# A gated two-branch layer: the output projection by seven products on halves, with the bias added to the input in DRAM

## The chip, the cores and the metric

The kernel runs on one core of a Trainium2 chip. The metric is the device time of one execution in microseconds (us), the median of several runs. The engines of the core are TensorE (PE: matrix products; its weight loads are shown apart as PEld), VectorE (DVE), ScalarE (ACT), GpSimd (POOL) and SyncE (SP). SP and POOL also issue DMA transfers, each through a queue of its own. "L389" stands at nearly every instruction of the profile, because a planner issues all of them from that one line; instructions are told apart by the tiles that they write and read.

## What is computed

The sizes are 1024 time steps (SEQ), 1024 channels (D_MODEL), one layer, float32 throughout. Cut to what matters here:

```python
h = x @ w_in + b_in                                   # 1024 x 6144
xa, za, xb, zb, ga, gb = split(h)                     # 1024 channels each
ya = rg_lru(causal_conv4(xa)) * silu(za)
yb = multiscale_pool(xb) * silu(zb)
merged = sigmoid(ga) * (ya @ w_proj_a) + sigmoid(gb) * (yb @ w_proj_b)
y = merged @ w_out + b_out                            # the output projection
out = layer_norm(alpha * x + y, ln_gain, ln_bias)     # alpha = 2 ** 0.25, mean and variance over the channels
```

## The kernel before

A float32 product is made of three matmuls: each operand is split into a high part in the matmul's own format (a cast on ScalarE) and the rest (a subtraction on VectorE, together `split`), and high x high, high x low and low x high are summed in a PSUM bank. One matmul takes a 128 x 128 block as weights and 512 columns as the moving operand.

Three stages follow one another on TensorE. In the first, the 24 groups of `order` (line 592: kinds A, G and B for the two branches and the gates) form `x @ w_in`, each by seven products on halves of the matrices in place of eight; the gate matmuls and the pooling run between them. `ya` and `yb` go to DRAM. In the second, the merge (from line 1188), the two projections are formed step by step, branch a and then branch b, each again by seven products (`steps`, line 1190: a in the order 1, 2, 6, 5, 3, 7, 4, then b in the order 1, 2, 6, 7, 5, 4, 3). A step is four groups `g` of twelve matmuls; its operands are loaded by `load` two steps ahead and split by `cast` one step ahead. The four quarters of `merged` lie in `sums[d // 2, h]` (d: block of 128 channels, h: half of the time steps); a quarter is complete when branch b's part is added, after b's steps 2, 5, 4 and 3 (`DONE`, line 1218). `split_m` (line 1239) then splits each block of it.

The sums of weights and inputs that the seven products need are made in DRAM by copies and adding DMAs on the POOL queue. They wait in a list (`jobs`, line 649), first in, first out. `run_jobs` (line 654) takes one after an A group and two after a G or B group, and each time POOL first copies one number that ScalarE copies out of the group (`pace`), so that the jobs don't run ahead. The list holds the sums of both projections' weights (`weight_sums`), the first and second part of the sums of ya (`input_sums1`, `input_sums2`, queued when its blocks 3 and 7 are stored) and the same of yb; the second part of yb is taken up in merge step ("a", 3).

The third stage is the output projection with the layer norm (from line 1338). It has no halves: for each block `s` of 128 time steps and each half `e` of the output columns `o_mm` (line 1357) sums over all eight channel blocks, 24 matmuls into one bank. First come eight blocks with e = 0, then eight with e = 1; the last bank is made in two pieces of 256 columns. `z` holds alpha * x + b_out, made by VectorE from a loaded x. `o_evac` (line 1365) adds the bank to z and takes the statistics of the sum (BATCH_NORM_STATS2); `o_norm` (line 1371) aggregates them, ScalarE takes the root, and four multiplies on VectorE (two for mean and gain, two for deviation and bias, 512 columns each) and two stores end a block. The weights of e = 0 are loaded and cast during the merge (`CASTS`, line 1281), those of e = 1 after it.

The order on every engine is set ahead of time by the planner (`Plan`, lines 162 to 397): TensorE and POOL keep the order of the program, and for the others a list schedule with guessed costs takes the task that is due first. A task is due when the first matmul that depends on it is, or, if none does, 40 us after its place in the program (1 us if it reads a PSUM bank or a tile of the small pool `e`). A task that becomes ready up to 3 us later and is due earlier makes a less urgent one wait (`HOLD`, line 361). Tiles come from pools with fixed numbers of buffers: 28 of kind x, 10 of kind w, 4 of kind r, 10 of kind k, 4 of kind e and 8 PSUM banks; a task that writes a new tile waits until one is free.

Of the kernel before, what the change touches and what calls it, by code (L numbers as in the profile page):

```python
# [16 lines left out]
P = 128  # L17
# [144 lines left out]
class Plan:  # L162
# [22 lines left out]
    def add(self, name, eng, op, args, kw):  # L185
# [6 lines left out]
        t.ins = refs[1:] if t.outs else refs  # L192
        t.deps, t.users, t.new = set(), [], []
# [61 lines left out]
    def order(self):  # L255
# [26 lines left out]
        state = {"table": None, "SP": 0.0, "ACT": 0.0, "POOL": 0.0, "pe": 0}  # L282
# [17 lines left out]
        def begin(t, now):  # L300
# [4 lines left out]
            t.start = now  # L305
            free[t.eng] = now + t.time
# [21 lines left out]
        while done < len(T):  # L328
            moved = True
            while moved:  # L330
# [10 lines left out]
                for e in ("ACT", "DVE", "SP", "POOL"):  # L341
# [60 lines left out]
def layer_kernel(ctx: ExitStack, tc: tile.TileContext, xq, x, w_in, par, wg, w_pool, wpa, wpb, w_out, rows, out):  # L402
# [324 lines left out]
    def a_gates(c, xc, xh, xl, sz):  # L727
# [388 lines left out]
    for i in range(1, len(order)):  # L1116
# [51 lines left out]
        if i >= 2:  # L1168
            run_jobs(1 if kind == "A" else 2, i, g.t7)
# [63 lines left out]
    sums, mh, ml = {}, {}, {}  # L1233
    HOMES = {2: (kt, kt), 5: (kt, xt), 4: (xt, rt), 3: (xt, xt)}
# [4 lines left out]
    def split_m(j, d, h):  # L1239
        if d % 2 == 0:  # L1240
            for k, t in enumerate((mh, ml)):
                f = HOMES[j][k]
                t[d // 2, h] = f(f"m{k}{d}{h}", F32R) if f is not kt else f(f"m{k}{d}{h}", F32R).rearrange("p (g s) -> p g s", g=2)
        sign = 1.0 if d < KQ else -1.0
        A.mul(of(mh, d, h), of(sums, d, h), sign)
        V.scalar_tensor_tensor(of(ml, d, h), of(sums, d, h), sign, of(mh, d, h).bitcast(F32), ALU.mult, ALU.subtract)

    wo = {}

    raw_wo = {}  # L1250


    def load_wo(e, p):
        raw_wo[e, p] = kt(f"wor{e}_{p}").rearrange("p (k n) -> p k n", k=2)
        nc.sync.dma_start(raw_wo[e, p], w_out[2 * p * P:2 * (p + 1) * P, e * H:(e + 1) * H].rearrange("(k p) n -> p k n", p=P))

    def cast_wo(e, p):
        h, l = ((wt if e == 0 else xt)(f"wo{t}{e}_{p}") for t in "hl")
        split(raw_wo.pop((e, p)), h, l)
        for k in range(2):  # L1260
            wo[e, 2 * p + k] = (h[:, k, :], l[:, k, :])
# [20 lines left out]
    for i, (n, j) in enumerate(steps):  # L1282
# [10 lines left out]
        for g in range(KQ):  # L1293
# [17 lines left out]
            if (n, j) in DONE:  # L1311
# [26 lines left out]
    for p in range(KQ):  # L1338
        load_wo(1, p)
        cast_wo(1, p)  # L1340
    rb = []
    for i in range(3):
        t = xt(f"row{i}", F32, (P, S))
        nc.sync.dma_start(t, rows[i:i + 1, :].to_broadcast((P, D)))
        rb.append(t)
    b_row, g_row, be_row = rb
    zt, stats = [], []
    for s in range(NK):
        t = xt(f"z{s}", F32, (P, S))
        nc.sync.dma_start(t, x[s * P:(s + 1) * P, :])  # L1350
        V.scalar_tensor_tensor(t, t, ALPHA, b_row, ALU.mult, ALU.add)
        zt.append(t)
        stats.append(const.tile([P, 4 if s == NK - 1 else 2, 6], F32, name=f"stats{s}"))
    eps = const.tile([P, 1], F32, name="eps")
    nc.gpsimd.memset(eps, EPS)

    def o_mm(ps, s, e, ks, sl=slice(0, H)):
        for k in ks:
            wh, wl = (w[:, sl] for w in wo[e, k])
            h, c = divmod(s * P, H)  # L1360
# [93 lines left out]
```

## Time and profile before

| | us |
|---|---|
| median of 3 runs (754.29 to 754.6) | 754.5 |
| the profiled execution, whole | 754.04 |
| its span, first to last instruction | 752.2 |
| TensorE busy | 742.5 (99%) |
| VectorE busy | 598.4 (80%) |
| ScalarE busy | 432.2 (57%) |
| GpSimd busy | 54.5 (7%) |

The profile is of one execution. Matmuls overlap in the pipeline, so one shows 389 ns while one starts about every 227 ns; the number of slots is what fills TensorE's time. The stage of the output projection runs from 656.42 us to the end. "Idle before" is an engine's idle time just ahead of an instruction, with what ended it.

### The profile page before, as it was taken

Reading aid. Unit: us, or ns where it says so; the run is one execution under the profiler, and the core shown is the slowest. Engines: PE = TensorE matmul, PEld = TensorE weight load, DVE = VectorE, ACT = ScalarE, POOL = GpSimd, SP = SyncE. Lnnn points to the kernel's source line nnn. Section 1 sums busy time; section 2 is a strip of 40 time slices with the busy share of each in tenths; the row PEclk is TensorE's granted clock in tenths of the full one; section 3 lists DMA queues with packets and bytes.
Section 4 is the critical chain, followed back from the end, with each engine's and each line's share of the span. In section 5 each row is a group of like instructions: output and inputs, shape, how many; then the busy total and the mean of one; then the engine's idle time right before and its main releaser. Section 6 shows DMA issues by size and latency. Waiting matters only on the chain.

```text
span 752.2 us, 8755 instructions
## 1 busy us (share of the span) xinstructions
PE 742.5 (99%) x3308; PEld 608.6 (81%) x3308; DVE 598.4 (80%) x740; ACT 432.2 (57%) x556; POOL 54.5 (7%) x101
## 2 busy tenths in 40 slices
PE   9999999999999999999999999999999999999996
PEld 6887888888788878878888888888888888888885
DVE  7898695959595969699977768779958896977587
ACT  7676969597787777788665444465543654230000
POOL 0160010101010100010011001000000000000000
PEclk9999999999999999999999999999999999999998
DMA  9146567657566647254278526898599996181022
GB/s 343 64 145 156 179 159 198 166 175 195 147 163 198 166 176 173 85 171 142 80 161 171 112 76 176 309 382 270 197 300 302 330 295 220 57 315 48 29 93 103
DMA packets 54730, 135.90 MB, mean 181 GB/s; under 512 B 3936, under 2 KB 7136, under 8 KB 54624
## 3 DMA queue, kind: packets, MB, share of 16 engines
q1 hardware_dynamic: 41248, 99.43, 37.9%
q0 software_dynamic: 12896, 35.65, 21.4%
q8 instruction: 26, 0.43, 0.2%
q10 hardware_dynamic: 544, 0.26, 0.1%
q14 instruction: 16, 0.13, 0.1%
HBM read 114.36 MB, written 56.62 MB: 227 GB/s over the span
## 4 chain that ended last, share of the span: by engine, by line
PE 95%; ACT 2%; DVE 1%; DMA 1%; issue 0%; DVEq 0%; ACTq 0%
PE ps_o L389 12%; PE a_B L389 11%; PE a_A L389 10%; PE a_G L389 10%; PE pa_a L389 6%; PE pa_b L389 6%; PE c_A L389 6%; PE c_B L389 5%; PE c_G L389 4%; PE ps_pool L389 3%; PE pc_b L389 3%; PE pc_a L389 3%; PE e_A L389 3%; PE ps_s L389 3%; PE e_G L389 3%; PE e_B L389 3%
## 5 line engine op out<-in xcount | busy, mean ns | idle before, releaser
L389 PE MATMUL ps_o<-woh,m 128*128 128x512 f32 (+1 forms) x272 | 80.5, 379 | 0.0
L389 ACT ACT_TABLE_LOAD x39 | 50.0, 1283 | 42.8 <-DVE mv L389 40.1
L389 PEld LDWEIGHTS ps_o<-woh,m 128*128 128x128 f32 x272 | 50.1, 188 | 10.1
L389 PE MATMUL ps_o<-wol,m 128*128 128x512 f32 (+1 forms) x136 | 51.5, 378 | 0.0
L389 DVE TENSOR_TENSOR i<-i,xc 128x1024 f32<-128x1024 f32 x8 | 9.8, 1225 | 38.6 <-ACT i L389 38.6
L389 POOL COPY paced<-pace 128x1 f32<-128x1 f32 x19 | 13.4, 706 | 259.6 <-ACT pace L389 259.6
L389 DVE SCALAR_TENSOR_TENSOR xc<-xp,par_sb,xc 128x1024 f32<-128x1024 f32 x24 | 30.8, 1282 | 0.5
L389 PEld LDWEIGHTS ps_o<-wol,m 128*128 128x128 f32 x136 | 25.6, 188 | 5.0
L389 DVE TENSOR_TENSOR z<-ps_o,z 128x512 f32<-128x512 f32 (+1 forms) x17 | 11.2, 659 | 18.8 <-PE ps_o L389 18.3
L389 PE MATMUL pa_a<-oh,oh 128*128 128x512 f32 x64 | 24.9, 389 | 0.0
L389 PE MATMUL pa_a<-oh,ol 128*128 128x512 f32 x64 | 24.9, 389 | 0.0
L389 PE MATMUL pa_a<-ol,oh 128*128 128x512 f32 x64 | 24.9, 389 | 0.0
L389 PE MATMUL pa_b<-oh,oh 128*128 128x512 f32 x64 | 24.9, 389 | 0.0
L389 PE MATMUL pa_b<-ol,oh 128*128 128x512 f32 x64 | 24.9, 389 | 0.0
L389 PE MATMUL pa_b<-oh,ol 128*128 128x512 f32 x64 | 24.9, 389 | 0.0
L389 ACT ACTIVATE m<-m 128x512 fp32r<-128x512 f32 x16 | 10.1, 632 | 25.3 <-DVE m L389 25.3
L389 ACT ACTIVATE i<-ps_g,par_sb 64x512 f32<-64x512 f32 x32 | 21.9, 685 | 3.3 <-DVE r L389 2.8
L389 ACT ACTIVATE sd<-mv,eps 128x1 f32<-128x1 f32 x8 | 2.4, 295 | 34.9 <-DVE mv L389 34.9
L389 ACT ACTIVATE r<-ps_g,par_sb 64x512 f32<-64x512 f32 x32 | 21.9, 684 | 0.5
L389 ACT ACTIVATE zb<-zb,par_sb 128x1024 f32<-128x1024 f32 (+1 forms) x16 | 14.9, 937 | 10.7 <-DVE zb L389 10.3
L389 PE MATMUL c_B<-x64h,wd_B 128*128 128x512 f32 x64 | 21.0, 389 | 0.0
L389 PE MATMUL c_A<-x64h,wd_A 128*128 128x512 f32 x64 | 21.0, 389 | 0.0
(435 smaller groups left out, 2380.9 us busy)
## 6 DMA issues: line engine op xcount, KB each, us to landing
sg<-sg SPq DMA_DIRECT2D x16, 512.0 KB, 3.6
ra_A<-in_w_in SPq DMA_DIRECT2D x8, 512.0 KB, 4.9
rb_A<-in_w_in SPq DMA_DIRECT2D x8, 512.0 KB, 3.8
ya<-r SPq DMA_DIRECT2D x8, 512.0 KB, 2.9
ra_B<-in_w_in SPq DMA_DIRECT2D x8, 512.0 KB, 3.4
rb_B<-in_w_in SPq DMA_DIRECT2D x8, 512.0 KB, 3.7
yb<-zb SPq DMA_DIRECT2D x8, 512.0 KB, 6.0
sgla<-sg SPq DMA_DIRECT2D x8, 512.0 KB, 6.3
```

The lines of the kernel that those rows point to most:

```text
L389: getattr(getattr(nc, t.op[0]), t.op[1])(*a, **k)
```

## The change

It replaces the third stage and what feeds it.

- The output projection becomes seven products on halves of `merged` and `w_out`, in the order 1, 6, 7, 5, 3, 4, 2 (`O_STEPS`), each four groups of twelve matmuls. Products 1, 6, 5 and 3 share the banks `a`, 7 and 4 the banks `c`; 2 has banks of its own, and its last group is made in two pieces of 256 columns. After products 1, 6, 7 and 5 the partial results are added to z as well, so a half block of z gets one to three adds in place of one.
- The sums of the weights are made in DRAM by eight more jobs (`output_sums`), queued when block 3 of ya is stored. The sums of `merged` are made on VectorE (`o_sums`, `o_sum4`), six operations of 1024 columns and two more. Of the splits of `merged` those of one quarter stay in the merge (`o_first`); the others become twelve splits of 1024 columns (`o_input`).
- b_out / alpha is added to x in DRAM by eight more jobs (`biased_input`, queued when block 7 of ya is stored), and the factor alpha goes into the first add. `run_jobs` takes two jobs after A and G groups and three after B groups.
- Except in the last block, the row sums come out of the adds (`accum_out`), and the sum of squares out of a Square on ScalarE over the whole block; BATCH_NORM_STATS2 goes there. The last block keeps its statistics.
- In the planner, a second output (`accum_out`) is tracked, and the test that makes a less urgent task wait takes account of how late TensorE is (`lag`).

```diff
+        if isinstance(kw.get("accum_out"), Ref):
 ...
-                        if any(u.due < t.due and when < end and u.due < end - HOLD for when, u in soon):
+                        if any(u.due < t.due and when < end and u.due + state["lag"] < end - HOLD for when, u in soon):
 ...
+    def output_sums():
+        a11, a12, a21, a22 = (w_out[H * k:H * (k + 1), H * i:H * (i + 1)].rearrange("(q p) n -> q p n", p=P)
+                              for i in range(2) for k in (1, 0))
+        p1 = summed("p1o", a21, a22)
+        p3 = summed("p3o", a11, a21)
+        p2 = summed("p2o", a11, p1)
+        src["w", "o"] = {1: a11, 2: a12, 4: a22, 5: p1, 6: p2, 7: p3, 3: summed("p4o", a12, p2)}
+    xb_d = [dram.tile([2 * P, D], F32, tag=f"xb{i}", name=f"xb{i}") for i in range(4)]
+    bias_d = dram.tile([1, D], F32, tag="bias", name="bias")
+    def biased_input():
+        for sl in HALF:
+            t = epool.tile([1, H], F32, tag="e", name=f"bias_{sl.start}")
+            nc.sync.dma_start(t, rows[0:1, sl])
+            A.mul(t, t, 1.0 / ALPHA)
+            nc.sync.dma_start(bias_d[:, sl], t)
+        for i in (2, 3, 0, 1):
+            jobs.append(lambda i=i: nc.gpsimd.dma_start(xb_d[i], x[2 * P * i:2 * P * (i + 1), :]))
+            jobs.append(lambda i=i: add_to(xb_d[i], bias_d.to_broadcast((2 * P, D))))
 ...
         store_y("a", c, hs)
         if c == KQ - 1:
             input_sums1("a")
+            output_sums()
         elif c == NK - 1:
             input_sums2("a")
+            biased_input()
 ...
-            run_jobs(1 if kind == "A" else 2, i, g.t7)
+            run_jobs(3 if kind == "B" else 2, i, g.t7)
 ...
+    om, ow = {}, {}
+    def o_first(d):
+        p, i = divmod(d - KQ, 2)
+        if i == 0:
+            om.setdefault(1, []).append([kt(f"o1{n}{p}", F32R).rearrange("p (g s) -> p g s", g=2) for n in "hl"])
+        high, low = (t[:, i, :] for t in om[1][p])
+        A.mul(high, of(sums, d, 1), -1.0)
+        V.scalar_tensor_tensor(low, of(sums, d, 1), -1.0, high.bitcast(F32), ALU.mult, ALU.subtract)
+    def o_sums(p):
+        b22, b12, b11 = sums[p, 0], sums[2 + p, 0], sums[2 + p, 1]
+        V.tensor_tensor(b11, b12, b11, ALU.subtract)
+        t2[p] = xt(f"t2o{p}", F32)
+        V.scalar_tensor_tensor(t2[p], b11, -1.0, b22, ALU.mult, ALU.subtract)
+        V.tensor_tensor(b12, b12, b22, ALU.add)
+    def o_sum4(p):
+        V.scalar_tensor_tensor(t2[p], t2[p], -1.0, sums[p, 1], ALU.mult, ALU.subtract)
+    def o_input(j, f):
+        raws = {6: t2, 7: [sums[2 + p, 0] for p in range(2)], 5: [sums[2 + p, 1] for p in range(2)],
+                3: [sums[p, 0] for p in range(2)], 4: t2, 2: [sums[p, 1] for p in range(2)]}[j]
+        om[j] = []
+        for p in range(2):
+            h, l = (f(f"o{j}{n}{p}", F32R) for n in "hl")
+            if f is kt:
+                h, l = (t.rearrange("p (g s) -> p g s", g=2) for t in (h, l))
+            split(raws[p], h, l)
+            om[j].append((h, l))
+    def load_wo(j, p, f):
+        raw = f(f"wor{j}_{p}")
+        if f is kt:
+            raw = raw.rearrange("p (k n) -> p k n", k=2)
+        nc.sync.dma_start(raw, src["w", "o"][j][2 * p:2 * p + 2].rearrange("k p n -> p k n"))
+        ow.setdefault(j, []).append(raw)
+    def cast_wo(j, p, f):
+        h, l = (f(f"wo{j}{t}{p}") for t in "hl")
+        split(ow[j][p], h, l)
+        ow[j][p] = h, l
 ...
-                    split_m(j, d, h)
+                    if j == 5:
+                        o_first(d)
+                    elif j == 4 and d % 2 == 1:
+                        o_sums((d - KQ) // 2)
             if (n, j, g) in CASTS:
+                k = CASTS.index((n, j, g))
                 with nc.within(SOON):
-                    cast_wo(0, CASTS.index((n, j, g)))
+                    cast_wo(1 if k < 2 else 6, k % 2, wt)
         if (n, j) in (("a", 4), ("b", 1)):
             for p in range(2):
-                load_wo(0, p if n == "a" else p + 2)
 ...
+    O_STEPS = (1, 6, 7, 5, 3, 4, 2)
+    zt = {}
+    for s in (4, 5, 6, 7, 0, 1, 2, 3):
+        zt[s] = xt(f"z{s}", F32, (P, S))
+        nc.sync.dma_start(zt[s], xb_d[s // 2][(s % 2) * P:(s % 2 + 1) * P, :])
 ...
+    def o_add(s, e, ps, sign, first, final, sl=slice(0, H)):
+        z = zt[s][:, e * H:(e + 1) * H][:, sl]
+        op = ALU.add if sign > 0 else ALU.subtract
+        if final and s != last:
+            V.scalar_tensor_tensor(z, z, ALPHA if first else 1.0, ps, ALU.mult, op, accum_out=acc[:, 2 * s + e:2 * s + e + 1])
+        elif first:
+            V.scalar_tensor_tensor(z, z, ALPHA, ps, ALU.mult, op)
+        else:
+            V.tensor_tensor(z, z, ps, op)
+        if final and s == last:
+            for k in (range(2) if sl == slice(0, H) else (sl.start // (H // 2),)):
+                i = 2 * e + k
+                V.bn_stats(stats[:, i, :], zt[s][:, i * H // 2:(i + 1) * H // 2])
 ...
+            nm, var = (const.tile([P, 1], F32, name=f"{n}{s}") for n in ("nm", "var"))
+            V.tensor_scalar(nm, acc[:, 2 * s:2 * s + 1], acc[:, 2 * s + 1:2 * s + 2], -1.0 / D, ALU.add, ALU.mult)
+            sq = kt(f"sq{s}")
+            A.activation(sq, zt[s], AF.Square, bias=nm, accum_out=var)
+            A.activation(sd, var, AF.Sqrt, bias=eps, scale=1.0 / D)
+            mean, op = nm, ALU.add
 ...
+    def operands(j):
+        f, w = (xt, xt) if j == 2 else (kt, wt)
+        if j != 6:
+            for p in range(2):
+                load_wo(j, p, rt)
+            for p in range(2):
+                cast_wo(j, p, w)
+        o_input(j, f)
+    a, c = ([None] * KQ for _ in range(2))
+    operands(6)
+    for i, j in enumerate(O_STEPS[:5]):
+        if j == 6:
+            for p in range(2):
+                o_sum4(p)
+        operands(O_STEPS[i + 2])
+        for g in range(KQ):
+            if j == 1:
+                a[g] = bank(f"oa_{g}")
+            elif j == 7:
+                c[g] = bank(f"oc_{g}")
+            ps = c[g] if j == 7 else a[g]
+            o_product(ps, j, g, j in (1, 7), j == 3)
+            if j == 1:
+                o_add(4 + g, 0, ps, 1, True, False)
+            elif j == 6:
+                o_add(4 + g, 1, ps, -1, True, False)
+            elif j == 7:
+                o_add(g, 1, ps, -1, True, False)
+            elif j == 5:
+                o_add(g, 1, ps, -1, False, True)
+            else:
+                o_add(g, 0, ps, 1, True, True)
+                o_norm(g)
+    for g in range(KQ):
+        o_product(c[g], 4, g, False, True)
+        o_add(4 + g, 1, c[g], -1, False, True)
+        pieces = (slice(0, H),) if g < KQ - 1 else (slice(0, H // 2), slice(H // 2, H))
+        for sl in pieces:
+            ps = bank(f"oe_{g}_{sl.start}")[:, 0:sl.stop - sl.start]
+            o_product(ps, 2, g, True, True, sl)
+            o_add(4 + g, 0, ps, 1, False, True, sl)
+        o_norm(4 + g)
```

## Rows read from the trace of the kernel before

**Rows 1.** the page, busy time of each engine, its share of the span, instructions

```profile
PE 742.5 (99%) x3308; PEld 608.6 (81%) x3308; DVE 598.4 (80%) x740; ACT 432.2 (57%) x556; POOL 54.5 (7%) x101
```

**Rows 2.** the chain of waits in order of time: start us, us, what

```profile
645.54 10.88 PE pa_b L389 x48
656.42 88.34 PE ps_o L389 x408
```

**Rows 3.** the bank of the output projection: one of its three operand pairs, with its shapes

```profile
L389 PE MATMUL ps_o<-wol,m x136: 281/389/398, 656.5 to 744.4; 128*128 128x512 f32 x120, 128*128 128x256 f32 x16
```

**Rows 4.** VectorE in order of time, one output block: start us, us, instruction, count

```profile
728.07 0.69 DVE L389 TENSOR_TENSOR z<-ps_o,z 128x512 f32<-128x512 f32 x1 [0.86 <-PE ps_o L389]
...
733.57 0.69 DVE L389 TENSOR_TENSOR z<-ps_o,z 128x512 f32<-128x512 f32 x1 [0.86 <-PE ps_o L389]
734.29 0.70 DVE L389 BATCH_NORM_STATS2 stats<-z 128x6 f32<-128x512 f32 x1
735.02 0.21 DVE L389 BATCH_NORM_AGGREGATE mv<-stats 128x2 f32<-128x12 f32 x1
735.27 1.42 DVE L389 SCALAR_TENSOR_TENSOR z<-z,mv,row 128x512 f32<-128x512 f32 x2
736.60 0.16 DVE L389 RECIPROCAL sd<-sd 128x1 f32<-128x1 f32 x1
736.79 1.42 DVE L389 SCALAR_TENSOR_TENSOR z<-z,sd,row 128x512 f32<-128x512 f32 x2
```

**Rows 5.** VectorE in order of time, behind the merge

```profile
659.73 3.70 DVE L389 SCALAR_TENSOR_TENSOR m<-m,m 128x512 fp32r<-128x512 f32 x6
663.34 3.49 DVE L389 TENSOR_TENSOR wol<-wor,woh 128x1024 fp32r<-128x1024 f32 x3
```

**Rows 6.** groups of one shape: count | busy us, mean ns | idle us before them, releaser

```profile
L389 DVE TENSOR_TENSOR z<-ps_o,z 128x512 f32<-128x512 f32 x15 | 10.4, 692 | 18.3 <-PE ps_o L389 17.8
...
L389 ACT CAST woh<-wor 128x1024 fp32r<-128x1024 f32 x8 | 8.3, 1051 | 9.4 <-DVE ol L389 6.2 <-DMA wor<-in_w_out 3.2
```

**Rows 7.** by window: PE, PEld, DVE, ACT, POOL busy, PE clock, DMA share, GB/s

```profile
420.00:450.00 30.00, 30.00 (x133) 24.75 (x132) 21.96 (x29) 13.30 (x19) 0.40 (x1) 1.00 0.21 61
490.00:500.00 10.00, 10.00 (x46) 8.29 (x45) 6.40 (x7) 5.35 (x6) 0.00 (x0) 1.00 1.03 380
656.42:744.77 88.35, 88.33 (x409) 73.12 (x407) 63.92 (x98) 9.24 (x15) 0.00 (x0) 1.00 0.32 116
```

**Rows 8.** GpSimd (POOL) in order of time: adding and copying DMAs as it issues them

```profile
379.76 1.05 POOL L389 DMA_DIRECT2D t2a<-ya  x1 [45.91 <-DMA ya<-r]
...
411.81 1.02 POOL L389 DMA_DIRECT2D t4a<-ya  x1 [9.93 <-DMA t4a<-ya]
...
454.68 0.66 POOL L389 DMA_DIRECT2D t1b<-yb  x1 [17.54 <-issue]
...
553.91 1.04 POOL L389 DMA_DIRECT2D t2b<-yb  x1 [79.13 <-DMA yb<-zb]
```

**Rows 9.** DMA issues: queue, count, KB each, median us from issue to landing

```profile
t4a<-ya POOLq DMA_DIRECT2D x2, 1024.0 KB, 11.9
...
row<-in_rows SPq DMA_DIRECT2D x3, 512.0 KB, 8.6
...
p2b<-in_wpb POOLq DMA_DIRECT2D x1, 1024.0 KB, 6.1
...
t2b<-yb POOLq DMA_DIRECT2D x1, 1024.0 KB, 14.4
```

**Rows 10.** POOL's queue on the page; then SP, ScalarE, SP in order of time

```profile
q0 software_dynamic: 12896, 35.65, 21.4%
...
490.18 0.37 SPq L389 DMA_DIRECT2D wa1r<-in_wpa  x1
...
499.18 1.05 ACT L389 CAST oh<-wa1r 128x1024 fp32r<-128x1024 f32 x1 [4.65 <-DMA wa1r<-in_wpa]
...
609.57 0.36 SPq L389 DMA_DIRECT2D xb4r<-t4b  x1
```

More of the change, by code (lines that the diff above doesn't have):

```diff
@@ L192, in add @@
         t.ins = refs[1:] if t.outs else refs
+        if isinstance(kw.get("accum_out"), Ref):
+            t.ins = [r for r in t.ins if r is not kw["accum_out"]]
+            t.outs.append(kw["accum_out"])
         t.deps, t.users, t.new = set(), [], []
@@ L281, in order @@
         pe = [t for t in T if t.eng == "PE"]
[L282 removed]
+        state = {"table": None, "SP": 0.0, "ACT": 0.0, "POOL": 0.0, "pe": 0, "lag": 0.0}
         def slots(t, now, commit=False):
@@ L305, in begin @@
             t.start = now
+            if t.eng == "PE":
+                state["lag"] = now - ideal[t.i]
             free[t.eng] = now + t.time
@@ L1230, in load_sg @@
             sgs[i] += [t[:, 0, :], t[:, 1, :]]
-    sums, mh, ml = {}, {}, {}
-    HOMES = {2: (kt, kt), 5: (kt, xt), 4: (xt, rt), 3: (xt, xt)}
+    sums, t2 = {}, [None] * 2
     def of(t, d, h):
         return t[d // 2, h][:, d % 2, :]
[L1239 to L1261, printed above, removed]
+    om, ow = {}, {}
@@ L1335, in layer_kernel @@
     merge.close()
[L1338 to L1353, printed above, removed]
+    O_STEPS = (1, 6, 7, 5, 3, 4, 2)
@@ L1354, in layer_kernel @@
+    zt = {}
+    for s in (4, 5, 6, 7, 0, 1, 2, 3):
+        zt[s] = xt(f"z{s}", F32, (P, S))
+        nc.sync.dma_start(zt[s], xb_d[s // 2][(s % 2) * P:(s % 2 + 1) * P, :])
+    g_row, be_row = (xt(f"row{i}", F32, (P, S)) for i in (1, 2))
+    nc.sync.dma_start(g_row, rows[1:2, :].to_broadcast((P, D)))
+    nc.sync.dma_start(be_row, rows[2:3, :].to_broadcast((P, D)))
+    acc = const.tile([P, 2 * NK], F32, name="o_acc")
     eps = const.tile([P, 1], F32, name="eps")
     nc.gpsimd.memset(eps, EPS)
[L1357 to L1360, printed above, removed]
-            a, b = (of(t, k, h)[:, c:c + P] for t in (mh, ml))
-            for i, (l, r) in enumerate(((a, wh), (a, wl), (b, wh))):
-                nc.tensor.matmul(ps, l, r, start=(k == 0 and i == 0), stop=(k == NK - 1 and i == 2))
@@ L1365, in o_evac @@
-    def o_evac(ps, s, lo, hi):
-        w = D // stats[s].shape[1]
-        nc.vector.tensor_tensor(zt[s][:, lo:hi], ps, zt[s][:, lo:hi], ALU.add)
-        for c in range(lo, hi, w):
-            nc.vector.bn_stats(stats[s][:, c // w, :], zt[s][:, c:c + w])
+    stats = const.tile([P, 4, 6], F32, name="stats")
+    last = NK - 1
+    def o_add(s, e, ps, sign, first, final, sl=slice(0, H)):
[11 more added lines that the diff above has]
+                V.bn_stats(stats[:, i, :], zt[s][:, i * H // 2:(i + 1) * H // 2])
@@ L1371, in o_norm @@
     def o_norm(s):
-        mv = const.tile([P, 2], F32, name=f"mv{s}")
         sd = const.tile([P, 1], F32, name=f"sd{s}")
-        nc.vector.bn_aggr(mv, stats[s])
-        nc.scalar.activation(sd, mv[:, 1:2], AF.Sqrt, bias=eps)
         sls = [slice(e * H, (e + 1) * H) for e in range(2)]
+        if s == last:
+            mv = const.tile([P, 2], F32, name=f"mv{s}")
+            V.bn_aggr(mv, stats)
+            A.activation(sd, mv[:, 1:2], AF.Sqrt, bias=eps)
+            mean, op = mv[:, 0:1], ALU.subtract
+        else:
[5 more added lines that the diff above has]
+            mean, op = nm, ALU.add
@@ L1398, in layer_kernel, with o_product @@
-    o_norm(s)
+    def o_product(ps, j, g, start, stop, sl=slice(0, H)):
+        for q in range(KQ):
+            mh, ml = (t[:, q % 2, g * P:(g + 1) * P] for t in om[j][q // 2])
+            wh, wl = (t[:, q % 2, sl] for t in ow[j][q // 2])
+            for i, (l, r) in enumerate(((mh, wh), (mh, wl), (ml, wh))):
+                nc.tensor.matmul(ps, l, r, start=start and q == 0 and i == 0, stop=stop and q == KQ - 1 and i == 2,
+                                 skip_group_check=True)
+    def operands(j):
[6 more added lines that the diff above has]
+        o_input(j, f)
```

22 lines of the change are left out of this document (5 added, 17 removed).

## The prediction

> **What bounds the kernel now.** The busy shares come first: TensorE works 742.5 us of a 752.2 us span and VectorE 80% of it [rows 1]. A TensorE this full means that the time is its instruction count plus what stands before and behind it. The chain of waits in order of time says the same for the end: from 656.42 us on there is one piece of 88.34 us, the 408 matmuls of the output projection, with nothing between them [rows 2]. The last one ends at 744.76 us and 7.4 us follow (add, statistics, normalization, store). So three questions decide: how many matmul slots go, whether something in front of them now makes TensorE wait, and whether VectorE is still done when TensorE is.
>
> The profiled execution took 754.04 us, 1.84 us more than its span; it lies 0.46 us under the median of 754.5 us. I work on the span and add both.
>
> **TensorE: the saving.** One of the three operand pairs has 120 full matmuls (512 columns) and 16 halves (256) [rows 3]; all three, 360 and 48. One output tile of 24 full ones takes 5.50 us, read from the starts of two successive adds, so 0.2292 us each [rows 4]; the halves are left with (88.34 - 82.5)/48 = 0.1215 us. Seven products on halves are 7 x 4 x 4 x 3 = 336 matmuls instead of 8 x 2 x 8 x 3 = 384; the last twelve are split in two, so 324 full and 24 halves. The product loop of the merge, which has the same shape (4 groups of 12), runs 48 in 10.88 us, 0.2267 each [rows 2]. New stage: 324 x 0.2267 to 0.2292 + 24 x 0.1215 = 76.4 to 77.2 us, a saving of 11.2 to 12.0. I take 11.6, since nothing tells which pace the new loop will have. (The Trainium skill, "TensorE: Matmul & The Clock Gate", part on matmul timing, gives N/2.4 + 2.5 ns, 215.8 ns here; the rows show 5% more, and by the page 48 matmuls would be worth 10.4 us.)
>
> **The start of the stage costs nothing.** Product 1 needs only the quarter that is complete after merge step 5, two steps (21.8 us) earlier, and weights cast inside the merge in the four places that held the old ones. Product 6 needs the sums after step 4 and has the 10.88 us of step 3 and the 11 us of product 1 as cover. Product 6 accumulates into the banks of product 1 and so waits for their adds; those have three groups (8 us) of slack. Only if VectorE were more than that behind would TensorE stand still. x and w_out arrive over SP with six more 512 KB loads, in a stretch where the DMA engines are 32% busy [rows 7].
>
> **VectorE: the tail.** Now it works 63.92 of the 88.35 us of the stage [rows 7], and 18.3 us of its idle time is waiting for the projection [rows 6]. In the merge, 12 of 16 splits go (12 x 0.617 = 7.4 us; six took 3.70 [rows 5]) and six 1024-wide sums come (six x 1.163 = 7.0; three such operations took 3.49 [rows 5]), so VectorE leaves the merge at about 663.3 as before. After that come: 24 operations of 1024 (12 low parts of inputs, 10 of weights, 2 sums) x 1.163 = 27.9; 27 adds from PSUM at 0.73 (start to start, 733.57 to 734.29 [rows 4]) and two halves at 0.45 = 20.6; two statistics of the last half, 0.9; seven normalizations of 0.2 + 1.33 + 0.19 + 1.33 = 3.05 (starts 735.02 to 736.79 [rows 4]) = 21.4. Gone are the eight scalings of x and most of the statistics. Sum 70.8 us, so done at 734.1; TensorE ends at 656.42 + 76.8 = 733.2. That is 0.9 us over, without one idle moment. Weights and inputs of a product can only be made when the product two ahead has let go of their buffers, so some idle is sure; the operands of the last product lie in other buffers and can fill most of it. The norms come late: four fall due in product 3 (11 us), which they overfill with its adds, and VectorE can hand back only about 0.8 us per tile (5.5 - 4.7) after that. What is left over stands in front of the last tile's chain. I take +1.5 us; bounds 0 (the planner fills all) and +6 (the 5 us of slack I count in products 7 and 5 stay empty).
>
> The adds with a row sum are a form that this trace does not have. If the sum is free the add stays at 0.73; if it is a small instruction of its own it is about the 0.19 of a reciprocal [rows 4], 15 x 0.19 = 2.9 us; if the accumulating form ran at half speed, 15 x 0.55 = 8 us more would go to the tail (a rival, below). I take the free form, since the statistics instruction also sums a row and costs what an add costs [rows 4]; the 2.9 lie inside the bound of 6.
>
> ScalarE gets 22 casts of 1.05 us [rows 6] (23 us), seven squares of about that length and the roots, about 32 us in 77: covered. New is that the first normalizing multiply writes over the tile which the square reads, so VectorE waits for ScalarE there, some 1.2 us per tile, with the other adds and norms queued behind it. Other tiles' work fills that except on the last but one; the last tile keeps the old statistics, so the final chain stays at 7.4 us. Should square and root want different tables, two loads per tile land on an idle engine; the tail sees one tile's worth at most, under 3 us.
>
> **The added DMA work on the POOL queue.** Sixteen jobs of 1 MB are added (four weight sums, x plus bias in four pieces, a copy and an add each). Counting the job list through the loop: with two jobs per group and three in the B groups the list runs empty at B4, as all must. In the front (200 to 345 us) nothing tight sees them. What counts is the order. The second input sums of branch a wait until 379.76 us for ya, and four adds later the queue is at 411.81 [rows 8]. Behind them now stand the eight jobs of x plus bias, and only then the first sums of branch b, which now start at 454.68 [rows 8]. A copy takes 6.1 us alone and an add 11.9 in company [rows 9]; four of each from 424 are 72 us, so 496, and the five b jobs (about 42 us) end near 538. The next job that matters starts at 553.91 [rows 8]: 16 us to spare. From 420 to 450 us the DMA engines are only 21% busy [rows 7], which takes in the first of them.
>
> What does collide is 480 to 510 us. SP loads the first merge operands there, with the engines at 1.03 of their share and 380 GB/s [rows 7]. The second half of the weights of step a1 is issued at 490.18 when its buffer falls free, lands 9 us later at 499.18 [rows 10], and is cast by 501.5 (1.05 and 1.22 us). Step a1 begins fourteen steps and one pool group (24 matmuls) ahead of 656.42, at 498.7, and its third group needs these weights 5.4 us later, at 504.1. Slack 2.6 us. One POOL job put into its flight costs 4.7 us (the queue's 34 jobs hold 21.4% of the span [rows 10], 161 us), so 2.1 us too late. Step a2 has more room. I take +2.0 us; bounds 0 and +6.4 (flight doubled).
>
> By the Trainium skill, "DMA: Bandwidth & Descriptors", section on queues, rings and completion order, each engine takes turns between queues packet by packet; by that rule the flight doubles to 18 us and TensorE stands 6.4 us, which is the upper bound above. No row shows one load alone beside an add.
>
> **Sum.** 752.2 - 11.6 + 1.5 + 2.0 = 744.1 us of span; + 1.84 = 745.9; + 0.46 = 746.4 against the median.
>
> **Rivals.**
> (a) Nothing comes back: POOL jobs are spread so that no weight load is late, and VectorE has no idle time. 752.2 - 11.6 + 0 to 1 = 740.6 to 741.6, so 742.9 to 743.9. For it: TensorE never waited for an operand in the merge. Against it: 0.9 us of overrun even at full use.
> (b) VectorE becomes the bound of the last stage: half-speed accumulating adds, or waits for the squares that nothing fills. 8 to 9 us of tail in place of 1.5: 753.4, with a clean front 751.4. For it: 70.8 us of work in 70 us. Against it: no operation in the trace with two inputs shows such a rate.
> (c) Slower: the POOL queue is late for branch b. The bias rows are one 4 KB row read 256 times; a row spread over 128 partitions takes 8.6 us for 512 KB [rows 9], so an add could take 17 instead of 12, and 14.4 was seen where the engines are full [rows 9]. The start of the adds into t2b (553.91) is what decides. It has the 16 us above. The last of that chain, t4b, is loaded at 609.57 [rows 10]; with some 7 us of flight and 5 us of casts it is ready at 622, for a step that starts two steps ahead of 656.42, at 634.7: 12 us more. So 28 us of delay are free, and every us beyond is a us of TensorE. At seven us more per job (8 x 7 = 56) TensorE stands 28 us: 746.4 + 28 = 774. It ends slower than before from 36 us of delay on, 4.5 us per job.
> (d) The change does not do what it says, for instance if the planner puts new waits ahead of casts: about the old time, 753 to 756.
>
> **Chances.** Forecast 0.57; (a) 0.18; (b) 0.12; (c) 0.08; (d) 0.05. Under 0.2% (1.5 us) a measurement of this kernel cannot tell a difference from none. Faster: forecast, (a) and the better part of (b), 0.84; same: the rest of (b) and part of (d), 0.07; slower: (c) and the odd case of (d), 0.09. Range: from the upper saving with nothing returned (752.2 - 12.0 + 2.3 = 742.5) to (b) with a clean front, 751.4, which takes in the forecast with the tail at its bound of 6 (750.9): 742.5 to 751.5. That leaves out (c), (d) and the worst of (b).
>
> **What would show it.** The chain: the piece at the end should be 76 to 77 us with 348 matmuls. TensorE's waits: if (c), idle before steps b6, b7 or b4 with a sum of branch b as releaser; if my 2 us are right, a wait in a1 or a2 for the cast of a weight. VectorE's timeline: idle time in the last stage falls from 24 us to under 6, and the last tile's add starts 1 to 3 us after the last matmul. It is wrong if the TensorE piece is over 79 us or if the tail behind the last matmul grows beyond 13 us.

## The result, and the profile after

The changed kernel takes 750.57 us (median of seven executions, 749.05 to 752.92) beside 754.57 us for the kernel before in the same comparison: a ratio of 0.9949, 95% interval [0.9931, 0.9967]. It is faster by 4.0 us, just under half of the 8.1 us that the prediction named (754.5 - 746.4). The profiled execution took 752.92 us (span 751.1), the slowest of the seven; what is read from its trace is therefore a little worse than the usual execution.

First the page: the busy line of each engine, as in [rows 1].

```profile
PE 735.8 (98%) x3248; PEld 601.0 (80%) x3248; DVE 607.8 (81%) x758; ACT 450.8 (60%) x579; POOL 66.9 (9%) x119
```

TensorE has 60 matmuls fewer, as planned (408 - 348 in the last stage). It is busy 6.7 us less and VectorE 9.4 us more. The chain of waits in order of time (start us, us, what) tells where the rest went; its last pieces answer to [rows 2].

```profile
489.88 15.71 DMA wa1r<-in_wpa
506.72 1.22 PE pa_a L394 x2
507.98 7.47 PE pa_a L394 x22
515.45 10.88 PE pe_a L394 x48
...
651.55 10.88 PE pa_b L394 x48
662.43 22.32 PE oa L394 x96
684.75 11.18 PE oc L394 x48
695.92 13.96 PE oa L394 x60
```

Two things are to be seen. The last stage starts at 662.43 us, 6.0 later than before (656.42), because a DMA now stands in the chain: the load of a weight of the first merge step (wa1r), 15.71 us from issue to landing. And the stage begins at 0.2325 us per matmul (22.32 / 96), where [rows 2] had 0.2267 in the merge.

TensorE's waits (us in total, times, longest), and TensorE in order of time around the longest:

```profile
PE pa_a L394 <- ACT oh L394: 3.0, 1, 3.0
```

```profile
503.29 0.39 PE L394 MATMUL pa_a<-oh,ol 128*128 128x512 f32 x1
506.72 0.80 PE L394 MATMUL pa_a<-oh,oh 128*128 128x512 f32 x1 [3.04 <-ACT oh L394]
...
509.00 0.63 PE L394 MATMUL pa_a<-ol,oh 128*128 128x512 f32 x1
509.42 0.63 PE L394 MATMUL pa_a<-oh,ol 128*128 128x512 f32 x1
...
513.21 0.40 PE L394 MATMUL pa_a<-oh,oh 128*128 128x512 f32 x1
513.45 0.39 PE L394 MATMUL pa_a<-ol,oh 128*128 128x512 f32 x1
```

Behind the 3.04 us of standing still the matmuls do not come at their old pace: 0.43 us from start to start until 512.4, then 0.23 again. The windows (from:to in us and their length, then columns as in [rows 7]) give the granted clock for it:

```profile
498.00:502.00 4.00, 4.00 (x20) 3.30 (x19) 1.76 (x2) 0.00 (x0) 0.00 (x0) 1.00 1.02 329
502.00:506.00 4.00, 1.68 (x8) 1.06 (x6) 0.00 (x0) 0.38 (x1) 0.99 (x2) 0.97 1.02 396
506.00:510.00 4.00, 3.25 (x7) 2.14 (x8) 2.62 (x3) 3.50 (x4) 0.00 (x0) 0.50 1.50 610
510.00:515.45 5.45, 5.45 (x20) 4.36 (x19) 1.60 (x2) 1.74 (x3) 0.00 (x0) 0.76 0.64 222
...
662.43:740.20 77.77, 77.77 (x349) 63.56 (x347) 67.74 (x109) 31.61 (x42) 0.00 (x0) 1.00 0.29 101
```

A granted clock of 0.50 is the lower of the two levels, 1.2 GHz; the 0.97 of 502 to 506 us puts its fall just ahead of 506, while TensorE still stood. The 24 matmuls from 506.72 to 515.45 took 8.73 us where the merge's pace makes it 24 x 0.2267 = 5.44. So the late weight costs 3.04 us of standing and 3.29 us of slow clock, 6.3 in all. The last stage is 77.77 us instead of 88.34.

GpSimd in order of time shows what was in the DMA engines during that flight; it answers to [rows 8].

```profile
404.47 0.91 POOL L394 DMA_DIRECT2D xb<-in_x  x1
...
468.33 1.54 POOL L394 DMA_DIRECT2D xb<-bias  x1 [13.97 <-DMA xb<-in_x]
...
469.37 2.37 POOL L394 DMA_DIRECT2D t1b<-yb  x1
487.75 1.03 POOL L394 DMA_DIRECT2D t1b<-yb  x1 [16.02 <-DMA t1b<-yb]
488.39 1.04 POOL L394 DMA_DIRECT2D t3b<-yb  x1
...
502.73 0.51 POOL L394 DMA_DIRECT2D t2b<-t1b  x1 [12.86 <-DMA t1b<-yb]
...
560.98 1.05 POOL L394 DMA_DIRECT2D t2b<-yb  x1 [57.26 <-DMA yb<-zb]
```

The eight jobs of input plus bias are issued from 404.47 to 468.33, and the first sum of branch b (t1b), which began at 454.68 before, begins at 469.37. Its adding DMA is in flight from 487.75 to 502.7, over all but the last 3 us of the load of wa1r (489.88 to 505.59); a copy (t3b) is issued at 488.39, and two more copies (t2b, t4b) at 502.73 and 503.22.

Last, VectorE behind the last matmul (which ends at 740.2), the counterpart of [rows 4]:

```profile
737.63 0.21 DVE L394 TENSOR_SCALAR nm<-o_acc 128x1 f32<-128x1 f32 x1
739.21 0.75 DVE L394 SCALAR_TENSOR_TENSOR z<-z,nm,row 128x512 f32<-128x512 f32 x1 [1.37 <-ACT sq L394]
739.88 0.68 DVE L394 TENSOR_TENSOR z<-z,oc 128x512 f32<-128x512 f32 x1
...
742.99 0.41 DVE L394 TENSOR_TENSOR z<-z,oe 128x256 f32<-128x256 f32 x1
743.33 1.40 DVE L394 BATCH_NORM_STATS2 stats<-z 128x6 f32<-128x256 f32 x4
...
746.58 1.41 DVE L394 SCALAR_TENSOR_TENSOR z<-z,sd,row 128x512 f32<-128x512 f32 x2
```

The span ends at 751.1, 10.9 us behind the last matmul, against 7.4 before. The last half's addition starts 2.8 us after the last matmul, and all four statistics of the last block run behind it; two of them belong to the half that was complete at 740.6.

Against the profiled execution before, the span so goes: merge starts 0.5 us earlier (498.08), + 6.3 for the late weight, - 10.6 for the matmuls, + 3.5 behind the last one; with 0.1 in the rest of the merge and the rounding of the pieces that is - 1.1, 752.2 to 751.1.

### The profile page after: what moved, and what is told of

Its sections match the earlier page's. It is cut to its first block, busy times and chain, and to the rows that moved or that the text cites. A ratio compares the mean times of both kernels' runs of the same rounds, so it can differ in the third digit from the quotient of the medians.

```text
span 751.1 us, 8794 instructions
## 1 busy us (share of the span) xinstructions
PE 735.8 (98%) x3248; PEld 601.0 (80%) x3248; DVE 607.8 (81%) x758; ACT 450.8 (60%) x579; POOL 66.9 (9%) x119
## 4 chain that ended last, share of the span: by engine, by line
PE 92%; DVE 4%; DMA 2%; ACT 1%; issue 0%; DVEq 0%; ACTq 0%
PE a_A L394 11%; PE a_G L394 10%; PE a_B L394 10%; PE pa_b L394 6%; PE c_B L394 6%; PE c_A L394 6%; PE pa_a L394 6%; PE c_G L394 5%; PE oa L394 5%; DVE z L394 4%; PE ps_s L394 3%; PE ps_pool L394 3%; PE pc_b L394 3%; PE pc_a L394 3%; PE e_A L394 3%; PE e_G L394 3%
## 5 line engine op out<-in xcount | busy, mean ns | idle before, releaser
L394 POOL COPY paced<-pace 128x1 f32<-128x1 f32 x21 | 10.1, 480 | 175.4 <-ACT pace L394 175.4
L394 PE MATMUL ps_pool<-mixh,wp 128*128 128x512 f32 x64 | 20.6, 394 | 0.0
L394 ACT ACTIVATE sq<-z,nm 128x1024 f32<-128x1024 f32 x7 | 8.0, 1149 | 19.9 <-DVE nm L394 19.9
L394 PE MATMUL e_A<-x,wah_A 128*128 128x512 f32 x64 | 19.7, 389 | 0.0
L394 PE MATMUL e_B<-x,wah_B 128*128 128x512 f32 x64 | 19.7, 389 | 0.0
L394 PE MATMUL c_G<-x64h,wd_G 128*128 128x512 f32 x56 | 18.4, 389 | 0.0
L394 DVE TENSOR_TENSOR_SCAN r<-a,i 128x1024 f32<-128x1024 f32 x8 | 18.3, 2283 | 0.1
L394 PEld LDWEIGHTS pa_a<-oh,oh 128*128 128x128 f32 x64 | 12.7, 198 | 6.1 <-ACT oh L394 3.5
## 6 DMA issues: line engine op xcount, KB each, us to landing
xb<-bias POOLq DMA_DIRECT2D x4, 1024.0 KB, 12.8
```

Source lines behind the costliest of these rows:

```text
L394: getattr(getattr(nc, t.op[0]), t.op[1])(*a, **k)
```

## Experiments

My theory after the result: the projection saved nearly what was forecast, and about five us of it were lost to the place of the eight input jobs in GpSimd's queue. Its rival: the jobs do no harm by themselves, and the stall has another cause, as the new weight sums or the changed pacing. Each run stands beside executions of the kernel before on its own chip; their medians are 754.28 to 754.37, so the times of different runs are set against each other directly.

**x1: no input jobs.** The input is loaded as it is, and the output bias is left out.

```diff
-            biased_input()
...
-        nc.sync.dma_start(zt[s], xb_d[s // 2][(s % 2) * P:(s % 2 + 1) * P, :])
+        nc.sync.dma_start(zt[s], x[s * P:(s + 1) * P, :])
```

> The changed kernel with z loaded straight from x and without the eight jobs that add the bias in DRAM (b_out is left out of the result). Theory A (the added POOL jobs stand beside the first weight loads of the merge): POOL's first sums of branch b start near 455 us again, the second half of the weights of step a1 lands near 499 in place of 505.6, TensorE has no stall in a1 and no stretch at half clock; the last stage starts 5 to 6 us earlier than in the profile of the changed kernel (662.4), and the median falls by 3 to 6 us to 745 to 747.5. Theory B (the planner's new order, not the jobs, puts the loads late): the stall stays and the time stays within 1.5 us of 750.6.

746.54 us (746.41 to 746.71), ratio 0.9897 [0.9884, 0.991]. No wait in the merge; t1b begins at 454.98, wa1r is issued at 489.74 and cast at 495.42, and the last stage starts at 655.96. The jobs are the cause of the 6 us; the new weight sums and the new pacing, which x1 keeps, are not.

**x2: the jobs alone, on the kernel before.** Sixteen jobs that nothing reads, and the new pacing.

```diff
+            output_sums()
...
+            biased_input()
...
-            run_jobs(1 if kind == "A" else 2, i, g.t7)
+            run_jobs(3 if kind == "B" else 2, i, g.t7)
```

> The kernel before with nothing but the sixteen new POOL jobs and the new pacing; nobody reads what they write. Theory A: TensorE stalls in step a1 of the merge for the same cast of weights, and the time rises by 3 to 7 us to 757.5 to 761.5. Theory B: no stall, 754 to 755.5.

764.38 us (763.42 to 768.28), ratio 1.0143 [1.0124, 1.0162]: 10 us slower, more than the 3 to 7 forecast, by the same mechanism. The chain of waits:

```profile
492.91 18.03 DMA wa1r<-in_wpa
510.96 1.05 ACT oh L389
512.06 1.22 PE pa_a L389 x2
513.32 7.12 PE pa_a L389 x22
...
667.50 87.96 PE ps_o L389 x408
```

Here the adding DMA of t1b is in flight from 492.83 to 507.1, the load takes 18.03 us, TensorE stands 6.6 us, and from 512 to 516 us its granted clock is 0.50 again; the 24 matmuls from 512.06 to 520.44 take 2.9 us more than at full clock. The last stage starts 11.1 us late. So in the kernel before the sixteen jobs in this place cost about as much as the seven products save on TensorE (10.6 us).

**x3: the input jobs first.** One line moved: the jobs go to the head of the queue, since input and bias are there from the start.

```diff
-            biased_input()
...
+    biased_input()
     weight_sums("a", wpa)
     weight_sums("b", wpb)
```

> The changed kernel with the eight bias jobs at the head of the list in place of behind the second sums of branch a; the same work, another place. Theory A: the jobs run by 150 us where the DMA engines have room, POOL's first sums of branch b start near 455 us, no stall in a1, median 745 to 747.5. Theory B: the stall stays, 749 to 752. If the extra jobs hurt wherever they stand, the front shows new TensorE waits instead.

745.84 us (745.59 to 748.34), ratio 0.9899 [0.9884, 0.9913]; it beats both kernels. The jobs are issued between 54 and 118 us, t1b begins at 454.30, wa1r lands in 5.2 us (9.0 in the kernel before, 15.7 in the changed one), TensorE waits for nothing in the merge. Two windows of it, the last stage and what follows:

```profile
655.23:733.00 77.77, 77.77 (x348) 63.56 (x347) 67.90 (x109) 31.63 (x42) 0.00 (x0) 1.00 0.28 99
733.00:743.80 10.80, 0.03 (x1) 0.00 (x0) 7.52 (x17) 0.29 (x1) 0.00 (x0) 0.70 0.26 97
```

With the late weight gone, two smaller differences to the forecast are left: 77.77 us for the matmuls rather than 76.8, and 10.8 behind them rather than 8.9. The next runs look at these.

**x4: tiles padded,** so that all operands of the matmuls lie at the same offset; the theory was that the slower pace comes from offsets. The small scalars of the normalization are packed into one tile as well.

```diff
-        return kpool.tile([P, w], dt, tag="k", name=name)
+        return kpool.tile([P, S + 32], dt, tag="k", name=name)[:, 0:w]
```

> The changed kernel with every tile of the k pool padded to 1056 floats, so that all tiles that matmuls read start at the same offset within 128 bytes (before, k tiles alternate between two offsets). In the profile of the changed kernel products 1, 6, 7, 5 run 48 matmuls in 11.16 us, the merge 10.88. Theory C (a k tile at the other offset makes a matmul's operand slower): those products run at 10.88, the stage is 1.2 to 1.5 us shorter, the median 749 to 749.5, with the stall in a1 still there. Theory D (the pace has nothing to do with the offset): 11.16 stays and the time is unchanged.

750.56 us (748.52 to 753.18), ratio 0.9954 [0.9939, 0.997]; 22.12 and 11.21 us for the pieces that took 22.32 and 11.18. The offset is not what sets the pace; its cause stays open. By chance the run says something on the clock. Its wa1r lands in 13.9 us, and its stall falls apart in three, with matmuls between:

```profile
PE pa_a L394 <- ACT um_a L394: 1.5, 1, 1.5
...
PE pa_a L394 <- ACT oh L394: 1.2, 1, 1.2
PE pa_a L394 <- DVE ol L394: 0.5, 1, 0.5
```

The granted clock stays 1.00 through 498 to 520 us, and the last stage starts at 659.78: 3.8 us later than in x1, of which the stalls are 3.2. The stalls without the slow clock cost little more than themselves.

**x5: statistics back on VectorE,** in x3: no row sums from accumulators, no Square.

```diff
-        if final and s != last:
-            V.scalar_tensor_tensor(z, z, ALPHA if first else 1.0, ps, ALU.mult, op, accum_out=acc[:, 2 * s + e:2 * s + e + 1])
-        elif first:
+        if first:
...
+        if final and s != last:
+            V.bn_stats(stats[s][:, e, :], z)
```

> The kernel of x3_bias_first (the changed kernel with the input's jobs at the head of GpSimd's queue, 745.84 us) with one part of the change undone: all eight blocks take their mean and variance from BN_STATS and BN_AGGR on VectorE again, no row sums from accumulators and no Square on ScalarE. Theory A (VectorE is the second limit of the last stage: it is busy 67.9 of the 77.8 us of TensorE and idle for some 8 us of the stage in all): VectorE gets 14 x 0.70 = 9.7 us of statistics, is rid of 14 accumulator reads of 0.08 us and of 4.6 us of waits for Square, so its end and the program's come 3 to 5 us later, 748.5 to 751. Rival B (the waits for Square, which stand in the same blocks, give back what the statistics took): 745.5 to 746.8. Under A the last stage's TensorE end stays near 733.0 in the trace and the piece behind it grows from 10.8 us to 13 to 16; under B it stays within 1 us of 10.8.

748.85 us (748.69 to 750.86), ratio 0.9932 [0.992, 0.9945]: 3.0 us more than x3. VectorE is busy 74.02 us of the 77.75 us of matmuls (67.90 in x3) and the piece behind them is 13.7 us. The statistics' move is worth 3 us, though the waits for Square (4.6 us in x3) eat part of it.

**x6: the last block first,** in x3: its additions and statistics are due at once.

```diff
+        late = 0.5 if g == KQ - 1 else nc.late
         o_product(c[g], 4, g, False, True)
-        o_add(4 + g, 1, c[g], -1, False, True)
+        with nc.within(late):
+            o_add(4 + g, 1, c[g], -1, False, True)
```

> The kernel of x3_bias_first with one edit of the order: the three additions of the last block and its four BN_STATS are due at once instead of at the planner's usual lateness, so that VectorE takes them ahead of the normalization of the block before. In x3 VectorE waits 1.37 us for the Square of that block while the last block's product 4 has been ready for about 2 us, and all four BN_STATS (1.40 us) run in a row behind the last matmul's addition. Theory A (the piece behind the last matmul, 10.8 us against 7.4 us in the kernel before, is an order in which the last block comes too late): the wait for Square is filled with the addition of product 4 and its statistics, the end comes 1.0 to 2.5 us earlier, 743.3 to 744.9. Rival B (it is the sum of VectorE's work that sets the end, and filling the wait only moves the block before to the end): 745.5 to 746.2.

745.13 us (744.88 to 745.29), ratio 0.9878 [0.9863, 0.9893], the fastest of all. VectorE in order of time now fills the wait for the Square of the block before:

```profile
730.65 0.21 DVE L394 TENSOR_SCALAR nm<-o_acc 128x1 f32<-128x1 f32 x1
730.78 0.68 DVE L394 TENSOR_TENSOR z<-z,oc 128x512 f32<-128x512 f32 x1
731.49 0.75 DVE L394 BATCH_NORM_STATS2 stats<-z 128x6 f32<-128x256 f32 x2
732.56 0.17 DVE L394 RECIPROCAL sd<-sd 128x1 f32<-128x1 f32 x1 [0.32 <-ACT sd L394]
```

The gain, 0.7 us, is below the forecast of 1.0 to 2.5: the order was one part of the long tail, and the amount of VectorE work behind the last matmul (6.6 us still, of 9.9) is the larger one. The time lies between the ranges of the two theories.

**x7: the planner's correction undone,** in x3. This part of the change, three lines in the planner, had no step in the prediction.

```diff
-                        if any(u.due < t.due and when < end and u.due + state["lag"] < end - HOLD for when, u in soon):
+                        if any(u.due < t.due and when < end and u.due < end - HOLD for when, u in soon):
```

> The kernel of x3_bias_first with the planner's correction for TensorE's lateness undone (the test whether an engine should be held free for a more urgent instruction counts with due times as they stand, as in the kernel before). Theory A: the correction only changes the order of a few instructions beside TensorE, and the time stays within 0.3% of 745.84, 744 to 748. Rival B (it is a working part of the change, since without it the planner keeps VectorE or ScalarE idle for instructions that TensorE's lateness has made less urgent): slower by 2 us or more, 748 to 752.

755.78 us (755.26 to 757.21), ratio 1.0019 [1.0011, 1.0028]: 9.9 us more than x3, and slower than the kernel before. That is rival B, by more than its range allowed. VectorE's waits in the last stage, x7 first, then x3:

```profile
DVE z L394 <- PE oa L394: 7.7, 10, 1.0
DVE z L394 <- PE oc L394: 2.7, 3, 1.0
```

```profile
DVE z L394 <- ACT sq L394: 4.6, 5, 1.4
...
DVE z L394 <- PE oa L394: 1.0, 2, 0.6
```

Without the correction the planner holds VectorE free for additions whose products are not there yet, ten times, and the normalizations are left for the end: 1.35 us more for the matmuls of the stage (one wait for a low part of an input, 0.6), 16.6 us behind them rather than 10.8, and a start of the stage 2.75 us later through small waits in the stages before. That sums to 9.9.

**x8: the bias on VectorE,** in x3: eight scalings as before, no input jobs.

```diff
-        nc.sync.dma_start(zt[s], xb_d[s // 2][(s % 2) * P:(s % 2 + 1) * P, :])
+        nc.sync.dma_start(zt[s], x[s * P:(s + 1) * P, :])
+        V.scalar_tensor_tensor(zt[s], zt[s], ALPHA, b_row, ALU.mult, ALU.add)
```

> The kernel of x3_bias_first with the bias back on VectorE as in the kernel before: the input is loaded as it is, eight 128x1024 scalar_tensor_tensor of 1.21 us scale it and add the bias row, the first additions are plain, and the eight jobs of GpSimd's queue are gone. Seven products, row sums and Squares stay. Theory A (VectorE is the second limit of the last stage, which is what the addition in DRAM relieves): 9.7 us of work come back, some of it ahead of the stage or in the 8 us in which VectorE is idle there; the end moves by 3 to 8 us, 749 to 754. Rival B (the scalings find idle time of VectorE before the first products are done, as in the kernel before, and the addition in DRAM earns nothing): 745.3 to 747.5.

747.02 us (746.79 to 748.47), ratio 0.9907 [0.9893, 0.992]: 1.2 us more than x3, within the rival's range. VectorE finds time for the scalings (75.40 us busy of the 77.50 us of matmuls; the profiled execution, 748.47 us, is the slowest of the four, and its merge starts 2.1 us later than that of x3, so only its last stage is read). So the addition in DRAM, which in its place in the changed kernel costs 4.7 us (750.57 - 745.84), is worth 1.2 in a harmless place, as long as the statistics stay off VectorE.

**x9: the planner's correction alone, on the kernel before,** the three lines of the diff.

```diff
+            if t.eng == "PE":
+                state["lag"] = now - ideal[t.i]
...
-                        if any(u.due < t.due and when < end and u.due < end - HOLD for when, u in soon):
+                        if any(u.due < t.due and when < end and u.due + state["lag"] < end - HOLD for when, u in soon):
```

> The kernel before with one part of the change done alone: the planner's correction for TensorE's lateness, three lines, which in x7_no_lag turned out to be worth 9.9 us of the changed kernel. Theory A (the correction is worth so much only because VectorE is nearly the second limit of the new last stage, where it otherwise is held idle for additions that TensorE's lateness has put off; in the old stage VectorE has 24 us of idle time, so nothing is gained): 753.3 to 755.3. Rival B (the correction helps by itself, through an earlier stage that is held up in the same way, and part of the change's gain has nothing to do with the projection): 749.5 to 752.5, with the last stage of the trace starting 2 us or more before 656.42.

753.32 us (753.03 to 754.22), ratio 0.9985 [0.9977, 0.9994]: 1.0 us faster, at the edge of the first theory's range. The last stage starts 0.9 us earlier (655.53) and is as long as before (88.35). So the correction is worth 1.0 us in the kernel before and 9.9 in the new one. That VectorE's lack of time is what makes the difference fits x7's waits, and is not shown further.

**x10: seven products alone,** x5 and x8 together: bias and statistics on VectorE, the correction kept.

> The kernel of x3_bias_first with both changes to VectorE's work undone together: bias added by eight scalings on VectorE as in x8_bias_on_vector (747.02 us) and all statistics by BN_STATS as in x5_bn_stats (748.85 us); seven products and the planner's correction stay. Theory A (VectorE is full in the last stage, so the two reliefs add up or more, each 3.0 and 1.2 us by itself): 750 to 754. Rival B (either relief alone frees the same idle time, or the two only move work that VectorE has time for): 748.5 to 749.8. In the trace A shows a TensorE end near 734 and a piece behind it of 14 to 18 us.

754.70 us (754.26 to 756.29), ratio 1.0004 [0.9995, 1.0013]: no gain at all, and 0.7 us above the range of theory A; the piece behind the matmuls is longer than its 14 to 18 us. The two windows:

```profile
655.38:732.95 77.57, 77.56 (x348) 63.52 (x347) 77.01 (x103) 22.45 (x26) 0.00 (x0) 1.00 0.27 96
732.95:752.50 19.55, 0.00 (x0) 0.00 (x0) 15.88 (x32) 0.88 (x3) 0.00 (x0) 0.57 0.28 107
```

TensorE is done at 732.95 as in x3. VectorE works 77.01 of the 77.57 us, has no time left, and all that is over (15.88 us) stands behind the last matmul. Eleven us of TensorE are exchanged for twelve of tail (10.8 and 12.1; the stage starts 1.0 us earlier than in the kernel before). The two reliefs cost 3.0 and 1.2 us when one is undone, 8.9 when both are: the first fills the idle time that is left, the second finds none.

## Why the prediction was half right

**Right: direction, range and mechanism of the loss.** The time lies inside 742.5 to 751.5. The wait in step a1 came where the prediction put it, at the cast of wa1r's second half, through a POOL job in its flight. Rival (c) did not occur: the input jobs ended near 481 us (the last is issued at 468.33, and such an add takes 12.8), not 496, and the adds into t2b began at 560.98, 7 us later than before, of 28 that were free. Of rival (b)'s two mechanisms one, accumulating adds at half speed, did not occur: they take 680 ns, and the accumulator read is an instruction of its own of 83 ns, 14 times, 1.2 us against the bound of 2.9. The other, waits for the squares, did: 4.6 us, but far from the 8 to 9 us of tail. ScalarE loads one table in the whole stage for Square and root together. The start of the stage costs nothing, as forecast.

**Wrong, and the step that failed: "I take +2.0" for the collision.** It was 6.3 in the profiled execution, and 4.7 between the medians with and without it (750.57 and 745.84, x3). One term was missing: TensorE, once it had stood still, went on at half clock for 5.7 us, which made 3.3 of the 6.3 us; the sum had nothing for it. Another was mis-sized: the flight was put at 9.0 + 4.7 = 13.7 us, one POOL job as the queue's mean share; it was 15.7 (18.0 in x2, 13.9 in x4). Both an adding DMA and a copy (t3b) were in it, and the engines were about as busy as before but moved less: from 490 to 500 us a share of 1.08 with 291 GB/s, where [rows 7] has 1.03 with 380. Without GpSimd's DMAs beside it the load takes 5.2 (x3) or 5.7 us (x1) in the new kernel, so they lengthened it by some 10 us, not 4.7. A third reading erred the other way: with the forecast's slack a flight of 15.7 us would mean 4.1 us of standing (15.7 - 9.0 - 2.6). It was 3.0, since the first matmul of the group waits for the cast alone (its releaser is ACT oh) and not for the subtraction behind it.

The forecast's upper bound was 6.4, for a standing of 6.4 us at a doubled flight; x2 had that case (18.03 us of flight, 6.6 of standing), and with the slow clock it cost 9.5. So the bound was too low as well. By the Trainium skill, "DMA: Bandwidth & Descriptors", section on queues, rings and completion order, engines take turns between the queues by packet. The 18 us that the prediction drew from this rule are met by x2's flight, the row-based 13.7 by x4's 13.9, and the changed kernel's 15.7 lies between; no run has the load beside one such DMA alone, so none decides between the two.

**Too large: the saving, 11.6.** It was 10.6 (88.34 - 77.77). I bounded the pace by 0.2267 and 0.2292; products 1, 6, 7 and 5 ran at 0.2325 to 0.233, products 3, 4 and 2 at about 0.228. The operands' offsets are not the cause (x4), and neither is how full VectorE is, since the pace is the same in x10 (22.31 for 96), where it has hardly any idle time. The cause stays open.

**Too small: the tail, + 1.5.** It was + 3.5, inside the bound of 6. The normalizations of the last two blocks stand there; 0.7 us of it is the order of the last block (x6). The forecast had VectorE's idle time fall under 6 us; it was 10.0 (77.77 - 67.74), 4.6 of it in the waits for Square.

**Not weighed at all: the planner's correction.** The prediction spoke of what the planner could fill ("0, the planner fills all") and did not ask what makes it do so. The three lines of the diff that do are worth 9.9 us of the new kernel (x7), more than all else but the matmuls. Without them the piece behind the last matmul is 16.6 us (x7), past the 13 at which the prediction called itself wrong.

In the sum, profiled execution against forecast for it: 752.9 - 745.9 = 7.0 us, of which 4.3 are the collision, 2.0 the tail, 1.0 the saving, and - 0.5 the earlier start of the merge, which no step forecast (the planner's correction alone starts the stage 0.9 us earlier, x9); 0.2 is rounding. At the median the gap is 4.2 us (750.57 - 746.4): 2.7 are the collision (4.7 against 2.0), and the rest is what x3, with the collision taken out, lies above the forecast without its 2.0 (745.84 against 744.4). That the usual execution of the changed kernel loses less than the profiled one because its clock does not fall is not shown; x4, profiled at 750.14, near that median, lost 3.8 us at full clock, which would fit.

What the change is worth by parts, from x3 with the jobs in a harmless place: seven products bring about 11 us of TensorE. They shorten the execution only with the planner's correction and with at least one of the two reliefs of VectorE: either relief alone leaves a gain of 5.5 (x5) or 7.3 us (x8), none leaves nothing (x10). Each of these undone takes 1.2 (bias), 3.0 (statistics), 8.9 (both) or 9.9 us (correction) back.

## What to carry to other kernels

When products are taken from the engine that bounds, look at once at the second engine of that stage: with 64 of 88 us busy it looked idle, and at 77 us it was full, so that the same saving brought nothing (x10) until work was taken off it. Added DMA jobs are judged by what they push, not by their own due time: the input jobs met their own needs with ease, but moved another sum into the flight of a tight weight load, and one moved line gave back 4.7 us. And TensorE's wait is priced with the clock behind it: here 3.0 us of standing in one piece cost 6.3, where 3.2 us in three pieces (x4) cost 3.8.

## What the runs showed of the hardware

- TensorE's granted clock fell to 0.50 (1.2 GHz) during a standing of 3.0 us (changed kernel) and of 6.6 us (x2), and came back 5.7 us after the restart in the first case (506.7 to 512.4) with matmuls running all the time; three stands of 1.5, 1.2 and 0.5 us with matmuls between left it at 1.00 (x4). Matmuls of 512 columns start 0.427 us apart at the low level and 0.227 at the high one. The Trainium skill, "TensorE: Matmul & The Clock Gate", section on the HAM clock gate (part 1), says that an idle TensorE falls back to 1.2 GHz, and the two longer stands agree.
- The same load of 512 KB on SP's queue took 5.2 (x3), 5.7 (x1) and 9.0 us (kernel before) among SP's own loads, and 13.9 (x4), 15.7 (changed kernel) and 18.0 us (x2) with a 1 MB adding DMA and a copy of GpSimd's queue in flight.
- An addition of 128x512 from PSUM with a row sum costs 680 ns on VectorE (692 without, [rows 6]) and an accumulator read of 83 ns; on ScalarE a Square of 128x1024 with a row sum costs 1149 ns and a read of 185 ns.
